# A block of halved products and its plain neighbours: which PSUM banks the plain pair takes, and where the halved pair's last product stands

## The chip, the cores and the metric

The kernel runs on one core of a Trainium2 chip. The metric is device time in microseconds (us) of one launch. Before the change the median of three runs is 963.95 us (963.66 to 964.03). Smaller is better.

TensorE (PE in the profile) multiplies and writes its sums into eight PSUM banks, numbered 0 to 7 here, each 128 partitions by 512 float32. VectorE (DVE) and ScalarE (ACT) read those banks, do the pointwise work and split operands. GpSimd (POOL) and SyncE (SP) mostly issue DMAs in this stretch. Each engine works through its own queue in order.

## The reference, cut to what matters

A decoder block with 512 tokens and 1024 channels: adaLN vector, a Mamba-2 mixer and a pooling mixer, then an MLP. The change touches the MLP alone:

```python
h = rmsnorm(x, norm_mlp_w[i]) * (1.0 + scale_f) + shift_f
x = x + gate_f * (jnp.square(jax.nn.relu(h @ w_up[i])) @ w_down[i])
return rmsnorm(x, norm_final_w)
```

`w_up` is 1024 x 4096 and `w_down` 4096 x 1024, all float32. Channels lie on the partitions and tokens on the free axis, so `h` is 8 blocks of 128 x 512, and the hidden layer 32 such blocks.

## The kernel before, in words

**Precision.** A float32 operand is split into a high part in a rounded format (`fp32r`) and a low part, the difference. A block product is then three matmuls: high by high, high by low, low by high (`mm3`, L154 to L158, and `product`, L870 to L874). The split is `two` (L835): a cast on ScalarE (L837), then a subtraction on VectorE (L838). Weights are split as they arrive, activations as they are made.

**Quarters.** The hidden layer is worked through in four quarters q = 0 to 3 of 8 blocks. In each, "up" jobs make the eight hidden blocks `us[0]` to `us[7]` (ReLU L1087, square L1088, split), and "down" jobs multiply them by `w_down` and add into the residual `x1`.

**Plain jobs and pairs.** A `Plain` job multiplies weight units as they are. A `Pair` job makes two output blocks at once by a Strassen-Winograd scheme over 2 x 2 halves: seven products of 12 matmuls of 256 columns (L874) in place of eight, with sums of weight parts S1 to S4 and sums of activation parts T1 to T4. A pair's products, by method:

- `lead` or `first`: A11·B11 into its accumulator bank `ac` (and A12·B21 ahead of it in a led pair, one that follows a plain job)
- `open`: S1·T1; `middle`: S2·T2, then VectorE adds (L971), and A12·B21; `third`: S3·T3, then VectorE adds (L978) from the left half of `ac` into its right half
- `close`: S4·B22, which completes the pair's first output block and hands it to `done(0, ...)`; then A22·T4 onto the left half of `ac`, which completes the second block, `done(1, ...)`, and frees `ac`

A22·T4 writes where the add of `third` reads, so it waits for L978. For an up pair `done` is `activated` (L1082): ReLU, square, split into `us`, and after the second block the T sums (L840 to L851) for the down pairs.

**Order of jobs** (L1228 to L1240): `up_first` (four plain up units), four plain up units (`up_plain`); then for every q a plain down job for output blocks 0 and 1 (`down_plain`), down pairs jj = 1 (the led one), 2, 3, and four up pairs for the next quarter. The last quarter ends with down pairs 1 and 2 and a plain job by token halves, `last_down`, for output blocks 6 and 7.

`run_jobs` (L992) writes them out. After a pair, at a plain job, the stream is: the pair's `close` (both products), the preparation of the next job (`prepare`: sum z, L906, and the split of S1 and A11; then `prepare_more`: rest of z, L917, and the split of S2 and S4), the plain job's matmuls, and then `prepare_rest` (the split of S3 and A12, and of A22).

`down_plain` goes over 16 blocks: k = 0 to 5 for its two outputs in turn, then k = 6, 7 for the first output and for the second. `us[6]` and `us[7]`, the last ones made, are thus read from the 13th block on.

**PSUM.** Banks 4 to 7 hold the pairs' first outputs, banks 0 and 1 (`AC`) the pairs' `ac`, banks 2 and 3 (`PU`) the plain jobs' sums. `up_first` uses 0, 1, 5 and 7; the four `up_plain` units take 2, 3, 2, 3; every `down_plain` takes 2 and 3. `Slots` hands out the longest free.

**SBUF slots.** Split weights lie in nine slots `HL`. The led pair's low part of S3 and A12 is written where the plain job's first unit had its high part, so that subtraction waits until TensorE is through with that unit's last block.

**The planner.** The stream is not issued as written. A planner places each engine's instructions in a queue beforehand: of those that are ready by its own estimates of durations, the one written first goes first, and work under `tc.high_priority()` ahead of that (the adds L971 and L978, DMAs, the split of plain units). `tc.issue_after(ins)` keeps an instruction behind `ins` on its engine. `mids` (L1080) lists the adds L971 and L978 as they are written.

Of the kernel before, what the change touches and what calls it, by code (L numbers as in the profile page):

```python
# [13 lines left out]
T = 512  # L14
# [48 lines left out]
def block_kernel(tc, xp, crow, arow, par, adaT, wstart, wz, wx, wpool_in, wgate, wpw, wbs, wbp, wout, wup, wdn, out):  # L63
# [3 lines left out]
    with (  # L67
# [764 lines left out]
        ut = [[[raws[p][:, 2 * i + k, :].bitcast(F32R) for k in range(2)] for i in range(2)] for p in range(2)]  # L832
        Y4S = Slots(lambda i, dt: slots("pad", 1, (P, T + 16), first=APART[i][0]).get(dt)[:, APART[i][1]:APART[i][1] + T], 4)

        def two(src, dst):  # L835

            act.copy(dst[0], src)  # L837
            dve.tensor_tensor(dst[1], src, dst[0].bitcast(F32), ALU.subtract)  # L838

        def sums(u1, u2, ts):  # L840

# [34 lines left out]
        class Pair:  # L876
# [17 lines left out]

            def keep(self, y, *names):
                hl = HL.get(F32R), HL.get(F32R)
                two(y, hl)
                for n, o in zip(names, (0, T)):
                    self.a[n] = tuple(x[:, o:o + T] for x in hl)
                    self.left[n] = hl  # L900

            def prepare(self):
                ya = self.y[0]
                self.a, self.left = {}, {}
                z = Z.get()
                dve.tensor_tensor(z[:, :T], ya[:, :T], ya[:, T:], ALU.add)  # L906
                if self.led:
                    yb = self.y[1]
                    dve.tensor_tensor(yb[:, :T], yb[:, :T], ya[:, T:], ALU.add)
                self.keep(ya, "S1", "A11")  # L910
                RL.put(ya)
                self.z = z
# [68 lines left out]
            def close(self):  # L981
                self.mul(self.c12, "S4", "B22")
                self.done(0, (self.c11, self.c12), 1)
                BE.put(self.be)
                self.mul(self.ac[:, :H], "A22", "T4")
                self.done(1, (self.ac,), -1)
                AC.put(self.ac)
# [4 lines left out]
        def run_jobs(jobs):  # L992

            last, todo = None, list(jobs)

            def pump():
                while todo and len(RL.free) >= todo[0].raws and (not isinstance(todo[0], Pair) or Y4.free):
                    todo.pop(0).fetch()

            pump()  # L1000
            jobs[0].prepare()
            pump()
            for n, job in enumerate(jobs):
                after = jobs[n + 1] if n + 1 < len(jobs) else None

                def ahead():
                    if after:
                        after.prepare()
                    pump()

                def more():
                    if isinstance(after, Pair):
                        after.prepare_more()

                def rest():
                    if isinstance(after, Pair):
                        after.prepare_rest()
                    pump()

                if isinstance(job, Pair):  # L1020
                    if not isinstance(jobs[n - 1], Pair):
                        if job.led:
                            job.lead()
                        else:
                            job.first()
                        job.open()
                    else:
                        job.first()
                    if last:
                        last.close()  # L1030
                    ahead()
                    job.middle()
                    more()
                    if isinstance(after, Pair):
                        after.open()
                    job.third()
                    last = job
                    rest()
                else:
                    if last:  # L1040
                        last.close()
                    last = None
                    ahead()
                    more()
                    job.run()
                    rest()
                    if job.after:
                        job.after()
                        pump()
# [49 lines left out]
        class Plain:  # L1099
# [10 lines left out]
                for u in self.units:  # L1110
                    u.prepare()

            def run(self):
                self.body([u.w for u in self.units])
                for u in self.units:
                    u.done()

        def up_first(w):

            ps = [AC.get(), AC.get(), banks[1], banks[3]]  # L1120
            for t0, t1 in HALVES:
# [31 lines left out]

        def up_plain(p, i):

            def f(w):
                ps = PU.get()
                for k in range(8):
                    mm3(ps, w[0][k], h2[k], k == 0, k == 7)
# [14 lines left out]

        def down_plain(q, js):

            def f(w):
                if q == 3 and 0 in js:
                    free([t for m in h2t for t in m])
                    sq.extend([S.get(), S.get()])  # L1180
                n = len(js)
                ps = [PU.get() for _ in js]
                order = [(k, i) for k in range(6) for i in range(n)] + [(k, i) for i in range(n) for k in (6, 7)]
                for k, i in order:
                    mm3(ps[i], w[i][k], us[k], k == 0, k == 7)
                for i, j in enumerate(js):
                    dve.scalar_tensor_tensor(x1[j], ps[i], mod[:, 40 + j:41 + j], x1[j], ALU.mult, ALU.add)
                    if q == 3:
                        squares(j)
                PU.put(*ps)  # L1190
            return Plain(loads(q, js), f)

        def loads(q, js):
# [11 lines left out]
                    squares(j)  # L1205
            return Pair(wdn[4 * jj + q], ub, f, jj == 1)

        def last_down(w):
            js = (6, 7)
            PU.free = [2, 3, 6, 7, 1, 0, 4, 5]  # L1210
            for t0, t1 in HALVES:
                for j in js:
                    ps = PU.get()
                    for k in range(8):
                        mm3(ps[:, t0:t1], w[j - 6][k], us[k], k == 0, k == 7, t0, t1)
                    x = x1[j][:, t0:t1]
                    dve.scalar_tensor_tensor(x, ps[:, t0:t1], mod[:, 40 + j:41 + j], x, ALU.mult, ALU.add)
                    squares(j, t0, t1, int(j == 7))
# [100 lines left out]
```

## Time and profile before

| | before |
|---|---|
| median of three runs | 963.95 us |
| the profiled execution, its own time | 962.53 us |
| its span, first to last instruction | 960.8 us |
| TensorE busy | 939.9 us (98%) |
| VectorE busy | 724.5 us (75%) |
| ScalarE busy | 542.5 us (56%) |
| mean granted TensorE clock | 0.995 |

All figures but the median are of one execution. "Busy" is the union of an engine's instructions; matmuls overlap, so a busy TensorE may still be slower than it could be, and its pace is read from the distance between starts. In a timeline row come the start, the duration, engine, line, operation, tiles (out<-in), the shape, and in brackets how long the engine sat idle before it and what ended that. Rows of equal instructions in a row are merged (xcount); the shape is then that of the first. In a row of windows come the stretch and its length, then for each engine its busy time and number of instructions, the granted TensorE clock, and the share and rate of the DMA engines.

### The profile page before, as it was taken

The numbers are of one execution on the slowest core, as the hardware profiler recorded it, in microseconds if no ns is written. First come the engines' busy times: TensorE is split into PE (matmuls) and PEld (weight loads), VectorE is DVE, ScalarE is ACT, GpSimd is POOL, SyncE is SP. The second block draws the span as 40 slices with busy tenths as digits, with TensorE's granted clock in tenths as the row PEclk, the third lists the DMA queues.
The fourth block names the chain that finished last, engine by engine and source line by source line (L and its number), as shares of the span: only waits on it lengthen the run. The fifth ranks groups of instructions, "written<-read, shape, count | busy, mean of one in ns | idle before, by whom it ended". The sixth has DMA issues, their size and how long they took to land.

```text
span 960.8 us, 14381 instructions
## 1 busy us (share of the span) xinstructions
PE 939.9 (98%) x5503; PEld 811.3 (84%) x5503; DVE 724.5 (75%) x1125; ACT 542.5 (56%) x893; POOL 126.1 (13%) x133
## 2 busy tenths in 40 slices
PE   8999999999999999999999999998999999999996
PEld 4777888888888888787888888996999899899896
DVE  7978868467766787987577565787769888977984
ACT  6479975667538542563412352585458547646853
POOL 0102321220312132300000000001111111111100
PEclk9999999999999999999999999999999999999998
DMA  9847333433253334446578364044586675676612
GB/s 364 304 133 186 124 102 121 132 111 110 75 158 113 98 106 131 154 154 200 179 262 278 119 210 132 23 114 106 134 201 153 149 195 148 164 188 174 169 30 88
DMA packets 70935, 146.34 MB, mean 152 GB/s; under 512 B 5521, under 2 KB 30353, under 8 KB 70866
## 3 DMA queue, kind: packets, MB, share of 16 engines
q1 hardware_dynamic: 64816, 134.41, 43.9%
q0 software_dynamic: 6048, 11.01, 7.5%
q8 instruction: 43, 0.70, 0.3%
q14 instruction: 26, 0.21, 0.1%
q10 hardware_dynamic: 2, 0.00, 0.0%
HBM read 143.17 MB, written 2.23 MB: 151 GB/s over the span
## 4 chain that ended last, share of the span: by engine, by line
PE 73%; DVE 12%; DMA 6%; ACT 5%; issue 3%; POOL 0%; SPq 0%; DVEq 0%; POOLq 0%; ACTq 0%
PE ps L874 17%; PE ps L156 16%; PE ps L158 16%; PE ps L157 16%; PE ps L328 4%; DMA d<-wdn 3%; DMA d<-cs_d 2%; DVE d L147 2%; DVE s L127 1%; PE ps L549 1%; DVE d L838 1%; ACT d L837 1%; DVE pad L631 1%; DVE d L172 1%; PE ps L529 1%
## 5 line engine op out<-in xcount | busy, mean ns | idle before, releaser
L156 PE MATMUL ps<-s,d 128*128 128x512 f32 (+1 forms) x896 | 343.5, 384 | 5.2 <-ACT s L1087 3.8
L157 PE MATMUL ps<-s,d 128*128 128x512 f32 (+1 forms) x896 | 339.2, 379 | 0.2 <-DVE s L127 0.2
L158 PE MATMUL ps<-s,d 128*128 128x512 f32 (+1 forms) x896 | 339.1, 379 | 0.0
L156 PEld LDWEIGHTS ps<-s,d 128*128 128x128 f32 x896 | 168.4, 188 | 40.2 <-ACT s L1087 4.2
L158 PEld LDWEIGHTS ps<-s,d 128*128 128x128 f32 x896 | 168.8, 188 | 32.0 <-issue 0.2
L157 PEld LDWEIGHTS ps<-s,d 128*128 128x128 f32 x896 | 168.6, 188 | 31.1 <-DVE s L127 0.7
L874 PE MATMUL ps<-s,d 128*128 128x256 f32 x1359 | 166.9, 279 | 0.7 <-DVE d L838 0.6
L874 PEld LDWEIGHTS ps<-s,d 128*128 128x128 f32 x1359 | 162.1, 188 | 2.0 <-DVE d L838 1.7
L147 DVE TENSOR_TENSOR d<-d,d 128x1024 fp32r<-128x1024 f32 x88 | 112.3, 1277 | 62.5 <-ACT d L146 57.6
L146 ACT CAST d<-d 128x1024 fp32r<-128x1024 f32 x88 | 92.0, 1046 | 115.5 <-PE ps L157 78.2
L837 ACT CAST d<-d 128x1024 fp32r<-128x1024 f32 x87 | 90.9, 1048 | 67.1 <-DVE d L917 23.7
L838 DVE TENSOR_TENSOR d<-d,d 128x1024 fp32r<-128x1024 f32 x87 | 105.8, 1223 | 25.1 <-PE ps L157 11.6
L172 DVE CUSTOM_DVE_ANT_0 d<-d,d,par_t 128x1024 f32<-128x1024 f32 x32 | 41.8, 1307 | 26.5 <-DMA d<-adaT 26.5
L891 POOL DMA_DIRECT2D d<-wdn x11 | 9.7, 883 | 312.2 <-DMA d<-wdn 261.5
L499 ACT ACTIVATE d<-d,ncs 128x128 f32<-128x128 f32 x128 | 39.9, 391 | 3.7 <-POOL d L495 3.6
L328 PE MATMUL ps<-s,d 128*128 128x512 f32 x168 | 40.1, 391 | 1.9 <-ACT s L316 1.9
L397 DVE SCALAR_TENSOR_TENSOR s<-ps,par_t,s 128x511 f32<-128x511 f32 (+2 forms) x54 | 39.7, 742 | 0.3
L328 PEld LDWEIGHTS ps<-s,d 128*128 128x128 f32 x168 | 31.4, 188 | 9.6 <-ACT s L316 2.4
L126 ACT CAST s<-s 128x512 fp32r<-128x512 f32 x32 | 19.7, 619 | 31.2 <-POOL s L511 18.7
L495 POOL TENSOR_SCALAR_AFFINE_SELECT d<-d 128x1024 f32<-128x1024 f32 x16 | 18.2, 1137 | 88.2 <-ACT cd L492 37.3
L127 DVE TENSOR_TENSOR s<-s,s 128x512 fp32r<-128x512 f32 x32 | 25.8, 808 | 4.6 <-ACT s L126 4.5
L874 PE MATMUL ps<-sz,d 128*128 128x256 f32 x198 | 28.4, 278 | 0.0
(231 smaller groups left out, 1236.5 us busy)
## 6 DMA issues: line engine op xcount, KB each, us to landing
d<-adaT SPq DMA_DIRECT2D x32, 512.0 KB, 4.2
d<-wup SPq DMA_DIRECT2D x32, 512.0 KB, 4.9
d<-wdn SPq DMA_DIRECT2D x32, 512.0 KB, 4.4
d<-wx SPq DMA_DIRECT2D x18, 512.0 KB, 3.6
d<-cs_d SPq DMA_DIRECT2D x16, 512.0 KB, 6.2
d<-wbs SPq DMA_DIRECT2D x16, 512.0 KB, 3.5
d<-wgate SPq DMA_DIRECT2D x16, 512.0 KB, 4.2
d<-wz SPq DMA_DIRECT2D x15, 512.0 KB, 3.7
```

The costliest lines, as they stand in the source:

```text
L146: act.copy(hi[:, :w], r[:, a:a + w])
L147: (low or dve).tensor_tensor(lo[:, :w], r[:, a:a + w], hi[:, :w].bitcast(F32), ALU.subtract)
L156: pe.matmul(ps, whi, xhi[:, t0:t1], start=start, stop=False)
L157: pe.matmul(ps, whi, xlo[:, t0:t1], start=False, stop=False)
L158: pe.matmul(ps, wlo, xhi[:, t0:t1], start=False, stop=stop)
L172: dve.tensor_tensor_reduce(r, r, cbc, 1.0, col("b_ada", j), ALU.mult, ALU.add, mod[:, j:j + 1])
L328: pe.matmul(first[u], w[u][i // 2], h[k][i % 2], start=k == 0 and i == 0, stop=k == 7 and i == 2)
L397: dve.scalar_tensor_tensor(t[:, sh:], ps[:, :T - sh], w(3 - sh), t[:, sh:], ALU.mult, ALU.add)
L499: act.activation(m[:, i, :], m[:, i, :], AF.Exp, bias=ncs[:, c, g * HG + i:g * HG + i + 1])
L837: act.copy(dst[0], src)
L838: dve.tensor_tensor(dst[1], src, dst[0].bitcast(F32), ALU.subtract)
L874: pe.matmul(ps, x, y, start=start and m == 0 and i == 0, stop=m == 3 and i == 2, skip_group_check=True)
```

## The change

1. **Banks.** `down_plain` of q = 0, which follows the plain up units, takes its two banks from `AC` (0 and 1); for q = 1 to 3, after a pair, it takes `PU` (2 and 3) as before.
2. **The pair's close is cut in two.** `close` keeps S4·B22 with `done(0, ...)`; a new `finish` has A22·T4, `done(1, ...)` and the release of `ac`. Between two pairs `finish` follows `close` at once, as before. Where a plain job follows, `finish` is handed to it: `down_plain` calls it after four of its blocks (k = 0 and 1 for both outputs), `last_down` after the eight blocks of its first half output.
3. **Edges.** In a led pair's `prepare` the sum z (L906) and the subtraction of the S1/A11 split are kept behind the newest add in `mids`, which is the add L978 of the up pair just ahead. At q = 0 no pair has run and `mids` is empty, so there is no edge. The cast of the split has none.

```diff
-        def two(src, dst):
+        def two(src, dst, late=None):
             act.copy(dst[0], src)
-            dve.tensor_tensor(dst[1], src, dst[0].bitcast(F32), ALU.subtract)
+            with tc.issue_after(late.ins) if late else nullcontext():
+                dve.tensor_tensor(dst[1], src, dst[0].bitcast(F32), ALU.subtract)
...
             def keep(self, y, *names):
                 hl = HL.get(F32R), HL.get(F32R)
-                two(y, hl)
+                two(y, hl, mids[-1] if mids and self.led else None)
...
                 z = Z.get()
-                dve.tensor_tensor(z[:, :T], ya[:, :T], ya[:, T:], ALU.add)
+                with tc.issue_after(mids[-1].ins) if mids and self.led else nullcontext():
+                    dve.tensor_tensor(z[:, :T], ya[:, :T], ya[:, T:], ALU.add)
...
                 self.mul(self.c12, "S4", "B22")
                 self.done(0, (self.c11, self.c12), 1)
                 BE.put(self.be)
+
+            def finish(self):
                 self.mul(self.ac[:, :H], "A22", "T4")
                 self.done(1, (self.ac,), -1)
                 AC.put(self.ac)
...
                     if last:
                         last.close()
+                        last.finish()
                     ahead()
                     job.middle()
...
                     if last:
                         last.close()
-                    last = None
                     ahead()
                     more()
-                    job.run()
+                    job.run(last.finish if last else None)
+                    last = None
...
-                ps = [PU.get() for _ in js]
+                at = PU if q else AC
+                ps = [at.get() for _ in js]
                 order = [(k, i) for k in range(6) for i in range(n)] + [(k, i) for i in range(n) for k in (6, 7)]
                 for k, i in order:
+                    if between and k == 2:
+                        between()
+                        between = None
                     mm3(ps[i], w[i][k], us[k], k == 0, k == 7)
...
-                PU.put(*ps)
+                at.put(*ps)
...
                     for k in range(8):
                         mm3(ps[:, t0:t1], w[j - 6][k], us[k], k == 0, k == 7, t0, t1)
+                    if between:
+                        between()
+                        between = None
```

`Plain.run`, `up_first`, `up_plain`, `down_plain`'s body and `last_down` get the argument `between` for this.

More of the change, by code (lines that the diff above doesn't have):

```diff
@@ L1111, in prepare, with run, up_first @@
                     u.prepare()
-            def run(self):
-                self.body([u.w for u in self.units])
+            def run(self, between):
+                self.body([u.w for u in self.units], between)
                 for u in self.units:
                     u.done()
-        def up_first(w):
+        def up_first(w, between):
             ps = [AC.get(), AC.get(), banks[1], banks[3]]
@@ L1154, in up_plain, with f @@
         def up_plain(p, i):
-            def f(w):
+            def f(w, between):
                 ps = PU.get()
@@ L1175, in down_plain, with f @@
         def down_plain(q, js):
-            def f(w):
+            def f(w, between):
                 if q == 3 and 0 in js:
@@ L1206, in down, with last_down @@
             return Pair(wdn[4 * jj + q], ub, f, jj == 1)
-        def last_down(w):
+        def last_down(w, between):
             js = (6, 7)
```

## The prediction

> **What bounds the kernel now.** I read the page's busy line and chain first, then TensorE's waits from 608 us on, where the MLP runs, and then the timelines around each wait.
>
> ```profile
> span 960.8 us, 14381 instructions
> PE 939.9 (98%) x5503; PEld 811.3 (84%) x5503; DVE 724.5 (75%) x1125; ACT 542.5 (56%) x893; POOL 126.1 (13%) x133
> PE 73%; DVE 12%; DMA 6%; ACT 5%; issue 3%; POOL 0%; SPq 0%; DVEq 0%; POOLq 0%; ACTq 0%
> ```
>
> TensorE is the bound: 98% busy and 73% of the chain that ended last. A change off it is worth only what it takes out of TensorE's waits.
>
> ```profile
> engine line waited for: us in total, times, longest us
> PE ps L156 <- ACT s L1087: 3.8, 1, 3.8
> PE ps L874 <- DVE ps L978: 3.2, 3, 1.1
> PE ps L874 <- DVE d L838: 0.6, 1, 0.6
> PE ps L778 <- ACT s L1167: 0.5, 1, 0.5
> ```
>
> In 352 us TensorE idles 8.1 us. The first two rows are the places that the diff touches: a plain matmul behind a ReLU, once, and A22·T4 (L874) behind the add L978, three times. The third is an up pair's own A12·B21 and the last the final norm; neither is touched.
>
> **Banks at q = 0.** TensorE's timeline around the long wait, then three windows:
>
> ```profile
> 659.46 0.39 PE L156 MATMUL ps<-s,d 128*128 128x512 f32 x1
> 660.37 0.40 PE L157 MATMUL ps<-s,d 128*128 128x512 f32 x1
> 664.58 0.60 PE L156 MATMUL ps<-s,d 128*128 128x512 f32 x1 [3.81 <-ACT s L1087]
> 676.13 2.99 PE L874 MATMUL ps<-s,d 128*128 128x256 f32 x24
> ...
> 660.00:664.60 4.60, 0.79 (x5) 0.32 (x3) 4.60 (x10) 2.40 (x6) 0.72 (x1) 1.00 0.70 159
> 664.60:668.00 3.40, 3.40 (x9) 2.65 (x10) 3.27 (x8) 2.35 (x4) 0.88 (x1) 0.54 0.67 138
> 745.90:748.00 2.10, 2.08 (x15) 1.99 (x16) 2.10 (x5) 1.55 (x4) 0.84 (x1) 1.00 0.63 95
> ```
>
> The plain down job runs from 659.46 to the led pair's first product at 676.13. Its second output wants bank 3, which the last up unit filled and whose ReLU (L1087) comes late. After the wait the granted clock is 0.54 for 3.4 us and a matmul takes 0.60 us (664.58) and not 0.39 (659.46). At full clock they start 0.229 us apart: at q = 1, shown below, 46 of them lie between 747.44 and 757.98. The job's 48 matmuls would then end at 659.46 + 48 x 0.229 = 670.46. So 5.67 us are lost, 3.98 in the gap (664.58 - 660.37 - 0.23) and 1.69 at the low clock. Banks 0 and 1 have been free since `up_first`, so this wait goes. What is late next:
>
> ```profile
> 663.62 0.40 ACT L837 CAST s<-s 128x256 fp32r<-128x256 f32 x1 [1.58 <-DVE s L842]
> 663.93 0.59 ACT L1087 ACTIVATE s<-ps 128x512 f32<-128x512 f32 x1
> 666.68 1.03 DVE L838 TENSOR_TENSOR s<-s,s 128x512 fp32r<-128x512 f32 x2
> 668.52 0.88 DVE L838 TENSOR_TENSOR s<-s,s 128x256 fp32r<-128x256 f32 x2
> 674.73 1.23 DVE L838 TENSOR_TENSOR d<-d,d 128x1024 fp32r<-128x1024 f32 x1 [5.33 <-PE ps L157]
> 675.87 1.40 DVE L1187 SCALAR_TENSOR_TENSOR xs<-ps,mod,xs 128x512 f32<-128x512 f32 x2
> ```
>
> The ReLU is late because ScalarE, in order, stood behind a cast that waited for VectorE; the change leaves that as it is. `us[7]` has its low part at 666.68 + 0.69 = 667.37, whatever TensorE does. Its first use is the second matmul of the 14th block, 659.46 + 40 x 0.229 = 668.62: 1.25 us to spare. Next is the low part of the led pair's A12, the row at 674.73. It waits for TensorE to leave its slot, 1.40 us ahead of 676.13, so then at 669.06. VectorE is through with the T sums at 668.52 + 0.88 = 669.40, so it runs to 670.63, and the lead's third matmul wants it at 670.46 + 0.24 = 670.70. Last, bank 0 goes on to the led pair's A11·B11: the first eviction L1187 would end near 671.4, and that product starts 12 matmuls of 0.118 us (24 in 2.83 us, at the end of the kernel, below) after the lead, at 671.9. All three fit, by 1.25, 0.07 and 0.5 us. **I take the whole 5.67 us**; bounds 2.5, if one of these chains slips by some 3 us in the new plan, and 5.67.
>
> The 1.69 us counts only if the low clock comes from the gap. The windows say so: 1.00 ahead, 0.54 right behind 3.8 us of idleness, but 1.00 behind the 1.03 us wait at 745.92. Were it otherwise, this part would be 3.98 and the total 1.7 less. The Trainium skill, page "TensorE: Matmul & The Clock Gate", Part 1, states that about 3.4 us of idleness puts the array at half clock and about 3.4 us of work restores it. By that rule any gap left shorter than this costs its own length alone; the trace agrees with its 3.8 and 1.03 us.
>
> **`finish` behind four blocks, q = 1 to 3.** TensorE at q = 1, then VectorE and two rows of ScalarE, then the windows of VectorE's packed stretch at q = 1 and q = 2:
>
> ```profile
> 744.51 0.39 PE L157 MATMUL ps<-s,d 128*128 128x512 f32 x1
> 745.92 1.68 PE L874 MATMUL ps<-s,pad 128*128 128x256 f32 x12 [1.03 <-DVE ps L978]
> 747.44 0.40 PE L158 MATMUL ps<-s,d 128*128 128x512 f32 x1
> 757.98 2.99 PE L874 MATMUL ps<-s,d 128*128 128x256 f32 x24
> ...
> 742.40 0.69 DVE L906 TENSOR_TENSOR d<-d 128x512 f32<-128x512 f32 x1
> 743.36 0.69 DVE L838 TENSOR_TENSOR s<-pad,s 128x512 fp32r<-128x512 f32 x1
> 744.30 1.22 DVE L838 TENSOR_TENSOR d<-d,d 128x1024 fp32r<-128x1024 f32 x1
> 745.44 0.43 DVE L978 TENSOR_TENSOR ps<-ps,pad 128x256 f32<-128x256 f32 x1
> 750.72 1.02 DVE L838 TENSOR_TENSOR s<-s,s 128x256 fp32r<-128x256 f32 x2
> 755.08 0.69 DVE L838 TENSOR_TENSOR pad<-pad,pad 128x512 fp32r<-128x512 f32 x1
> 756.58 1.23 DVE L838 TENSOR_TENSOR d<-d,d 128x1024 fp32r<-128x1024 f32 x1 [0.81 <-PE ps L157]
> 747.69 0.59 ACT L1087 ACTIVATE s<-ps 128x512 f32<-128x512 f32 x1
> 748.18 1.04 ACT L837 CAST d<-d 128x1024 fp32r<-128x1024 f32 x1
> ...
> 741.79:755.77 13.98, 12.95 (x75) 11.15 (x74) 13.97 (x27) 9.97 (x19) 2.60 (x3) 1.00 0.68 167
> 823.52:837.49 13.97, 12.92 (x76) 11.12 (x75) 13.97 (x27) 9.95 (x19) 2.60 (x3) 1.00 0.68 170
> ```
>
> A wait costs 745.92 - 744.51 - 0.23 = 1.18 us; three (3.2 us idle in the list of waits), 3.54. The add L978 stands behind the led pair's split (744.30), and ahead of that its z (742.40): the two that the edges move. Behind four blocks, of which two matmuls had run by then (the one at 747.44 is the third of a block), A22·T4 starts at 744.51 + 11 x 0.229 = 747.03, and L978 without the split ends near 744.7. So the wait goes with 2.3 us of cover, and would go even with no edges.
>
> Whether 1.18 us then reach the end is VectorE's matter: it works 13.97 of 13.98 us, and at q = 2 just so. Its next appointment is the led pair's A12 low part (756.58), which today starts 0.81 us after VectorE is free (755.08 + 0.69 = 755.77) and is wanted two matmuls into the lead. With the lead at 757.98 - 1.18 = 756.80 that is 757.04, so it must start by 755.8. If the pack ends at 755.77 still, all 1.18 us are kept. But z leaves 0.6 us at 742.40 (0.69 less the 0.09 by which neighbours overlap) that may stay empty, since the row at 743.36 waits for a cast on ScalarE; then the pack ends at 756.37 and the lead waits 0.6, so 0.58 is kept. Another row could fill it, as the planner takes what is ready. The bounds are 0 (the pack a whole wait later) and 1.18. **I take 0.85 a quarter, 2.55 in all**, between these two readings.
>
> The second half of the up pair's work comes later: A22·T4 ends at 748.6 instead of 747.6, so its ReLU (747.69) and `us[7]` (low part at 750.72 + 1.02 = 751.74) come about 1.0 later, 752.7. The 14th block's second matmul, the job's 41st, wants it at 744.51 + 39 x 0.229 + 1.41 = 754.85: 2.1 us to spare. Behind that ReLU on ScalarE stand the T casts, whose products come after the lead. The moved z and split serve A11 and S1, not read before 758.2; only S1/A11's raw slot, freed up to 1.8 us later (z's 0.6 and its own 1.14), lets a DMA go later on SP's queue. That is the third down pair's first load, not summed until the led pair's seven products have run, 7 x 1.41 = 9.9 us. So I count nothing; with that cover gone it would cost those 1.8 us.
>
> **`finish` in `last_down`.**
>
> ```profile
> 938.18 0.87 PE L874 MATMUL ps<-sz,pad 128*128 128x256 f32 x6
> 939.60 0.28 PE L156 MATMUL ps<-s,d 128*128 128x256 f32 x1
> 945.25 0.59 PE L778 MATMUL ps<-s,ones 128*128 128x256 f32 x2
> 941.62 0.69 DVE L1171 TENSOR_TENSOR s<-s,s 128x512 f32<-128x512 f32 x1 [0.70 <-ACT s L1170]
> ```
>
> A22·T4 at 938.18 waits for nothing, so there is nothing to win. Moved behind one half output (half of 939.60 to 945.25, 2.83 us), its squares' add would end at 941.62 + 0.69 + 2.83 = 945.1, with the other output's half to add behind it, while the norm's L778 wants the sum at 945.25. I charge 0.15; bounds 0 and 0.5.
>
> **Sum**: 5.67 + 2.55 - 0.15 = 8.07, say 8.0. The profiled execution had 962.53 (span 960.8 and 1.7 around it) and goes to 954.5; the median lies 1.42 above it, so 963.95 - 8.0 = **956.0**.
>
> **Rivals.** *All waits go whole*: 5.67 + 3.54 = 9.2, 954.7. For it: one row put into z's place is enough. Against: the pack has no spare. *VectorE takes it back*: it ends a wait later, the three quarters keep nothing, 963.95 - 5.67 = 958.3; the packed windows speak for it. *A chain slips at q = 0*: of the margins 1.25, 0.07 and 0.5 one is missed by 3 us, 5.0 in all, 959.0. *It does not do what it says*: the wait for bank 3 reappears whole for `us[7]` or A12, and 963.9 stays; that needs `us[7]` at 674 in place of 667.4, and no row holds it so long. *Slower*: the last unit's chain is planned behind the preparation. In the stream `finish` now stands behind z, S1/A11 and S2/S4, so on ScalarE two casts of 1.04 and on VectorE two subtractions of 1.14 (744.30 to 745.44) may go first. At q = 1 to 3 `us[7]` slips by up to 4.4, past its 2.1: a wait of 2.3 in place of 1.18, 3.4 lost in all. If the new plan does the same to the last plain up unit at q = 0, 4.4 past 1.25 is 3.15 idle, with 1.69 at the low clock behind it, and 0.8 of the 5.67 is left. Together 963.95 + 3.4 - 0.8 = 966.5. It decides from `us[7]` at 754.85 (q = 1) and 668.62 (q = 0). Against it: most of the preparation is ready, and placed, before that ReLU could start.
>
> **How the numbers follow.** Chances: forecast 0.52, all whole 0.12, VectorE 0.15, slip at q = 0 0.10, no change 0.06, slower 0.05. About 0.2% (1.9 us) is what a measurement tells from no change. The first four are faster, 0.89; then 0.06 and 0.05. The range reaches from below "all whole" to above the slip, 953.6 to 960.0, and leaves out the last two.
>
> **What would show it.** No wait of L156 on L1087 and granted clock 1.00 through the plain job at q = 0, whose 48 matmuls take about 11.0 us; no wait on L978; L906 and the led split behind L978. A wait of the lead's L874 on VectorE's L838 at q = 1 to 3 tells how much VectorE takes back: 0.3 each by my sum, 0 or 1.2 by the rivals. A wait of L156 to L158 on L838 at the 14th block would prove me wrong on `us[7]`.

## The result and the profile after

The changed kernel takes **958.43 us** (median of four runs, 957.45 to 959.96) against 963.99 us for the kernel before beside it (four runs, 963.66 to 965.29). The ratio is 0.9941, with a 95% interval of 0.9922 to 0.9960: 5.7 us less, between 3.9 and 7.5 (5.6 by the medians). The forecast was 956.0, so 8.0 less, and the time lies inside its range of 953.6 to 960.0. Measured again beside the experiments, the changed kernel had a ratio of 0.9924 (0.9904 to 0.9944), 7.3 us less, between 5.4 and 9.3. Two slow executions, one of e1 (1034 us, its only traced one) and one of e2 (4613 us), are left out of all medians, ratios and intervals, and e1's trace isn't read.

The page of the profiled execution, which took 959.38 us, shows the span, the busy line and the shares of the chain that ended last:

```profile
span 957.7 us, 14382 instructions
PE 942.1 (98%) x5503; PEld 813.6 (85%) x5503; DVE 725.1 (76%) x1125; ACT 542.4 (57%) x893; POOL 126.2 (13%) x133
PE 76%; DVE 12%; DMA 5%; ACT 4%; issue 2%; POOL 0%; SPq 0%; DVEq 0%; POOLq 0%; ACTq 0%
```

TensorE is still the bound, with the same 5503 matmuls. Its waits from 605 us on (L874, L838, L978 and L1087 of before are L875, L839, L980 and L1092 now):

```profile
engine line waited for: us in total, times, longest us
PE ps L875 <- DVE d L839: 1.2, 3, 0.5
PE ps L778 <- ACT s L1172: 0.5, 1, 0.5
```

Both rows that the diff aimed at are gone, 3.8 us behind the ReLU and 3.2 us behind the add. One has come in their place: 1.2 us in three waits on VectorE's subtraction. The final norm's 0.5 us stand as they were.

**At q = 0.** A window over the plain down job's 48 matmuls, TensorE's row that ends it, and two rows of VectorE inside it:

```profile
662.41:673.40 10.99, 10.99 (x50) 9.01 (x48) 10.77 (x21) 7.03 (x13) 1.74 (x2) 1.00 0.64 143
673.40 2.99 PE L875 MATMUL ps<-s,d 128*128 128x256 f32 x24
...
669.50 1.03 DVE L839 TENSOR_TENSOR s<-s,s 128x512 fp32r<-128x512 f32 x2
672.14 1.22 DVE L839 TENSOR_TENSOR d<-d,d 128x1024 fp32r<-128x1024 f32 x1
```

The job takes 10.99 us at clock 1.00, where it took 16.67 (659.46 to 676.13): 5.68 us less. `us[7]` has its low part at about 670.2, and the 14th block's second matmul wants it at 662.41 + 40 x 0.229 = 671.57. The led pair's A12 low part is done at 673.36 (672.14 + 1.22), ahead of the third product's start at 673.64. All nine traces with the new banks (this one and those of e4 to e7 and e9 to e12) have 10.99 us here.

**At q = 1.** TensorE at the lead, then rows of VectorE's pack ahead of it:

```profile
753.81 0.40 PE L875 MATMUL ps<-s,d 128*128 128x256 f32 x2
754.67 2.86 PE L875 MATMUL ps<-s,d 128*128 128x256 f32 x22 [0.47 <-DVE d L839]
...
739.04 0.69 DVE L839 TENSOR_TENSOR s<-pad,s 128x512 fp32r<-128x512 f32 x1 [1.09 <-ACT s L837]
740.11 0.68 DVE L839 TENSOR_TENSOR pad<-pad,pad 128x512 fp32r<-128x512 f32 x1
741.64 0.43 DVE L980 TENSOR_TENSOR ps<-ps,pad 128x256 f32<-128x256 f32 x1
752.46 0.68 DVE L908 TENSOR_TENSOR d<-d 128x512 f32<-128x512 f32 x1
753.40 1.22 DVE L839 TENSOR_TENSOR d<-d,d 128x1024 fp32r<-128x1024 f32 x1
```

A22·T4 no longer waits for the add (741.64). But the lead's third matmul waits 0.47 us for A12's low part, which VectorE begins at 753.40 with no gap ahead of it. At q = 2 and 3 the wait is 0.49 and 0.25 us. From the product at 737.89 us on (740.62 before) and from the like ones at q = 2 and 3, a dozen products into the lead, the same 105 products take 18.19, 18.22 and 17.98 us where they took 18.89, 18.71 and 18.95. Without what a quicker pace of some of them saved (0.15 us in each quarter now, 0.21 at q = 2 before; the pace is explained below), the quarters keep 0.55, 0.55 and 0.83 us of the 1.2 us each.

So the change's own places give 5.68 + 1.93 = 7.6 us in this pair of traces. The spans differ by 3.1 only. Two things that the diff doesn't touch make up the difference.

**The start.** Rows of the chain that ended last, from the first 36 us, of the kernel before:

```profile
1.73 5.42 DMA d<-xp
14.57 5.06 PE ps L328 x21
20.10 4.78 PE ps L328 x21
```

The same of the changed kernel:

```profile
1.72 6.90 DMA d<-xp
16.02 6.67 PE ps L328 x21
23.16 4.78 PE ps L328 x21
```

The first transfer took 1.48 us longer. Then 21 products took 6.67 us and not 5.06: the granted clock from 14 to 22 us was 0.79, and 1.00 before. That is 3.06 us (23.16 - 20.10) lost ahead of everything that was changed.

**The pace.** Two windows of 40 us in a stretch of 256-column products in the trace of before:

```profile
845.00:885.00 40.00, 40.00 (x355) 40.00 (x354) 31.05 (x45) 22.30 (x34) 7.37 (x9) 1.00 0.73 182
685.00:725.00 40.00, 40.00 (x342) 40.00 (x341) 31.75 (x46) 22.14 (x34) 6.08 (x7) 1.00 0.74 177
```

And in the changed kernel's:

```profile
845.00:885.00 40.00, 40.00 (x342) 40.00 (x341) 31.76 (x47) 22.13 (x34) 6.11 (x7) 1.00 0.76 179
```

TensorE is busy throughout at clock 1.00, and yet 355 products pass in one window and 342 in another: 0.1133 us or 0.1178 us from start to start, taken product by product. The quick pace saves 1.5 us in 40. The kernel before had it from 822.5 to 826.3 and from 839.7 to 901.1 us, the changed kernel only in three stretches of 3.8 us (from 737.9, 819.0 and 900.2). Counted product by product from 605 us on, against 0.1178 us, it saved 3.0 us before and 0.8 after.

The sum of it: 7.6 less, 0.6 less for the old wait on L838 that is gone too, 3.1 more at the start, 2.2 more by the pace: 2.9, and the spans show 3.1.

### The profile page after: what moved, and what is told of

It is laid out like the page before. It is cut to its first block, busy times and chain, and to the rows that moved or that the text cites. A ratio compares the mean times of both kernels' runs of the same rounds, so it can differ in the third digit from the quotient of the medians.

```text
span 957.7 us, 14382 instructions
## 1 busy us (share of the span) xinstructions
PE 942.1 (98%) x5503; PEld 813.6 (85%) x5503; DVE 725.1 (76%) x1125; ACT 542.4 (57%) x893; POOL 126.2 (13%) x133
## 4 chain that ended last, share of the span: by engine, by line
PE 76%; DVE 12%; DMA 5%; ACT 4%; issue 2%; POOL 0%; SPq 0%; DVEq 0%; POOLq 0%; ACTq 0%
PE ps L875 18%; PE ps L156 17%; PE ps L157 16%; PE ps L158 16%; PE ps L328 4%; DMA d<-wdn 3%; PE ps L549 1%; DVE d L147 1%; DMA d<-cs_d 1%; DVE s L127 1%; DVE s L839 1%; ACT d L837 1%; DVE d L839 1%; PE ps L529 1%; DVE pad L631 1%
## 5 line engine op out<-in xcount | busy, mean ns | idle before, releaser
L875 PE MATMUL ps<-s,d 128*128 128x256 f32 x1359 | 169.2, 280 | 1.3 <-DVE d L839 1.2
L875 PEld LDWEIGHTS ps<-s,d 128*128 128x128 f32 x1359 | 163.7, 188 | 3.2 <-DVE d L839 2.9
L839 DVE TENSOR_TENSOR d<-d,d 128x1024 fp32r<-128x1024 f32 x87 | 105.8, 1222 | 17.6 <-ACT d L837 10.6
L328 PE MATMUL ps<-s,d 128*128 128x512 f32 x168 | 41.7, 403 | 1.9 <-ACT s L316 1.9
L328 PEld LDWEIGHTS ps<-s,d 128*128 128x128 f32 x168 | 32.5, 195 | 10.1 <-ACT s L316 2.4
L875 PE MATMUL ps<-sz,d 128*128 128x256 f32 x198 | 28.7, 279 | 0.0
```

The lines of the kernel that those rows point to most:

```text
L328: pe.matmul(first[u], w[u][i // 2], h[k][i % 2], start=k == 0 and i == 0, stop=k == 7 and i == 2)
L875: pe.matmul(ps, x, y, start=start and m == 0 and i == 0, stop=m == 3 and i == 2, skip_group_check=True)
```

## The experiments

The kernels ran in three groups, each beside the kernel before: e1 to e4 and e7 to e10 on one chip (medians of before 964.98 and 965.58 us), e5, e6, e11 and e12 on another (965.05). "Less" is what the ratio makes of the median before; it can differ by 1 us from the difference of the medians. "Waits" is TensorE's time lost from 605 us on in the profiled execution, start to start beyond 0.1178 us (256 columns) or 0.229 us (512 columns), the low clock included; "pace" is what the quick pace saved there; "start" is the first transfer and the clock from 14 to 22 us. Waits less pace, taken from a kernel's time between the first product counted and the end of its span, leave 346.4 to 346.6 us in every trace of this table, so the two account for what differs there.

| kernel | median us | ratio (95%) | less, us | waits | pace | start |
|---|---|---|---|---|---|---|
| before (profiled first) | 963.95 | | | 14.2 | 3.0 | 5.42, 1.00 |
| changed (the result) | 958.43 | 0.9941 (0.9922 to 0.9960) | 5.7 | 6.0 | 0.8 | 6.90, 0.79 |
| e1 banks | 959.66 | 0.9935 (0.9916 to 0.9954) | 6.3 | | | |
| e2 finish | 963.93 | 0.9986 (0.9970 to 1.0001) | 1.4 | 13.3 | 0.9 | 6.83, 1.00 |
| e3 edges | 961.75 | 0.9959 (0.9943 to 0.9975) | 4.0 | 14.5 | 5.4 | 6.46, 1.00 |
| e4 banks, finish | 958.12 | 0.9922 (0.9908 to 0.9937) | 7.5 | 6.4 | 1.1 | 6.35, 1.00 |
| e9 changed, again | 958.32 | 0.9924 (0.9904 to 0.9944) | 7.3 | 7.5 | 5.3 | 6.31, 0.79 |
| e7 z later | 955.07 | 0.9895 (0.9873 to 0.9916) | 10.1 | 5.3 | 0.6 | 6.78, 0.79 |
| e10 cast later | 956.46 | 0.9909 (0.9896 to 0.9923) | 8.8 | 6.2 | 1.0 | 5.24, 1.00 |
| e8 shorter gap | 963.16 | 0.9973 (0.9958 to 0.9988) | 2.6 | 12.5 | 3.3 | 6.21, 0.79 |
| e12 z later, again | 956.42 | 0.9912 (0.9889 to 0.9934) | 8.5 | 6.5 | 4.3 | 1.00 |
| e11 z and cast later | 954.10 | 0.9885 (0.9866 to 0.9903) | 11.1 | 4.9 | 4.1 | 5.95, 0.79 |
| e5 banks, edges | 956.17 | 0.9904 (0.9886 to 0.9923) | 9.3 | 6.1 | 3.0 | 5.32, 0.79 |
| e6 end put back | 956.81 | 0.9911 (0.9890 to 0.9932) | 8.6 | 6.8 | 2.9 | 4.69, 1.00 |

e12's chain starts with another transfer, so it has no first figure.

### e1: the banks alone

```diff
-                ps = [PU.get() for _ in js]
+                at = PU if q else AC
+                ps = [at.get() for _ in js]
...
-                PU.put(*ps)
+                at.put(*ps)
```

> Part 1 alone: the plain down job at q = 0 takes banks 0 and 1; close is not cut, no edges. Theory (the bank wait and the low clock behind it are one loss, and nothing takes it back): 5.7 us less than before, 958.3; in the profile no wait on the ReLU at q = 0, its 48 matmuls in 11.0 us at clock 1.00, and the three waits of about 1.05 us on the add of the third product as before. Rival (the gap goes but the low clock stays, or another chain takes over): 4.0 us less or fewer, and a granted clock below 1.00 in that stretch or a new wait at the 14th block.

6.3 us less (4.4 to 8.1). The 5.67 us of the prediction's first step lie within it, and 4.0, the rival's, lies just outside. For the trace, the nine others with these banks stand in: 48 matmuls in 10.99 us at clock 1.00, and no wait on the ReLU.

### e2: `finish` behind four blocks alone

The changed kernel with `at = PU` and without the two edges (`two(y, hl)`, and z with no `issue_after`).

> Part 2 alone: close cut in two, A22·T4 behind four plain blocks, no edges, banks as before. Theory (finish alone covers the late add, the edges are not needed for that): no wait on the add; since z and the led pair's split stay in VectorE's early gap, the pack ends earlier and the lead waits less for the A12 low part than the 0.47, 0.49 and 0.25 us of the changed kernel; 2.5 to 3.5 us less than before, 960.5 to 961.5. Rival (the edges carry the gain): a wait on the add stays, under 1 us less than before.

1.4 us less, between 2.9 less and 0.1 more: a miss. The list of waits from 605 us on, without the norm's row:

```profile
PE ps L156 <- ACT s L1091: 4.5, 1, 4.5
PE ps L875 <- DVE d L839: 1.5, 3, 0.7
```

The wait on the add is gone, so four blocks cover it without the edges, as the prediction said. The lead pays 1.5 us in its place, and not less than in the changed kernel, as I had expected with z in its old place. And at q = 0, where this kernel keeps the old banks, the wait behind the ReLU has grown from 3.8 to 4.5 us; what came behind it:

```profile
667.00:670.00 3.00, 3.00 (x8) 2.31 (x7) 2.84 (x7) 1.88 (x5) 0.88 (x1) 0.50 0.34 48
```

The job's 48 matmuls run from 660.64 to 678.61, 17.97 us in place of 16.67. So some 1.3 us of what this part won it lost at q = 0: 0.7 by a plan that put that ReLU later, the rest because the low clock lasted 6.8 us and not 3.4. With the new banks nothing waits there and the loss can't arise: the parts don't add up.

### e3: the edges alone

The changed kernel with `at = PU`, and `last.finish()` right behind `last.close()` as before.

> Part 3 alone: z and the led pair's low part behind the add of the third product; A22·T4 right behind S4·B22 as before, banks as before. Theory (the add is late because the split of 1.14 us and z of 0.6 us stand ahead of it): the add runs about 1 us earlier, the three waits of 1.05 us fall to 0.3 or less; VectorE's later work takes some back at the lead; 1 to 3 us less than before. Rival (the add is late for other work): waits stay near 1 us and the time is that of before.

4.0 us less (2.4 to 5.5), above what I expected. Its trace explains that only in part. The waits from 605 us on are no fewer than before, and those on the add stay above the 0.3 us of the theory:

```profile
PE ps L156 <- ACT s L1093: 3.8, 1, 3.8
PE ps L875 <- DVE d L839: 1.8, 2, 1.2
PE ps L875 <- DVE ps L980: 1.6, 2, 0.9
```

TensorE's rows at q = 1, with VectorE's row and ScalarE's cast behind them:

```profile
741.29 4.27 PE L875 MATMUL ps<-s,d 128*128 128x256 f32 x34 [1.18 <-DVE d L839]
746.31 1.68 PE L875 MATMUL ps<-s,pad 128*128 128x256 f32 x12 [0.76 <-DVE ps L980]
...
743.22 0.69 DVE L839 TENSOR_TENSOR s<-pad,s 128x512 fp32r<-128x512 f32 x1 [1.64 <-ACT s L837]
...
740.62 1.04 ACT L837 CAST d<-d 128x1024 fp32r<-128x1024 f32 x1 [1.81 <-DMA d<-wdn]
```

At q = 0 the gap is that of before, 3.8 us, but the low clock again lasted 6.8 us and the job took 17.49. The quick pace ran from 678 to 731 and from 759 to 820 us and saved 5.4 us. TensorE came early to places where VectorE wasn't ready, and gave some of it back in waits. VectorE itself stood 1.64 us because ScalarE stood behind the led cast, whose transfer was late. That every execution of e3 has so much of the quick pace isn't shown: only one was traced.

### e4: banks and `finish`, no edges

```diff
-                two(y, hl, mids[-1] if mids and self.led else None)
+                two(y, hl)
...
-                with tc.issue_after(mids[-1].ins) if mids and self.led else nullcontext():
-                    dve.tensor_tensor(z[:, :T], ya[:, :T], ya[:, T:], ALU.add)
+                dve.tensor_tensor(z[:, :T], ya[:, :T], ya[:, T:], ALU.add)
```

> Parts 1 and 2 without the edges. Theory (edges only shift VectorE's work and finish covers the add alone): at least as fast as the changed kernel, 5.7 + 2.5 to 3.5 less than before, 954.8 to 955.8 against a kernel before of 964. Rival (edges needed): slower than the changed kernel by 1 us or more, with waits on the add at q = 1 to 3.

7.5 us less (6.1 to 8.9): as fast as the changed kernel, though 0.7 short of what I wrote. Its list of waits, the norm's row left out:

```profile
PE ps L875 <- DVE d L839: 1.4, 4, 0.4
```

No wait on the add without the edges. And the lead waits 0.39, 0.31 and 0.21 us at q = 1 to 3 (the fourth wait is at q = 0), though z and the split stand where they stood before the change. So z's emptied place, from which the prediction took its 0.6 us, isn't needed for the lead's wait.

### e9: the changed kernel again

> The changed kernel once more, beside the others on one chip. Theory (the waits are gone in the plan, the rest is drawn anew in each execution): TensorE shows the same waits of the lead's first A22·T4 product on VectorE, 0.2 to 0.5 us at q = 1 to 3, and none on the ReLU at q = 0, whose 48 matmuls take 11.0 us; but the first x transfer takes nearer 5.4 than 6.9 us, the clock from 14 to 22 us is nearer 1, and the span falls by 2 to 3 us against 957.7; the median lies 957.5 to 959.0, 5.5 to 7 below the kernel before. Rival (start-up and pace are tied to the new order of the work): first transfer 6.9 us, clock 0.8 from 14 to 22 us, span within 0.5 of 957.7, and the fast pace of 0.1133 us per product in the same three stretches.

7.3 us less. A window of 40 us:

```profile
685.00:725.00 40.00, 40.00 (x356) 40.00 (x354) 32.57 (x49) 24.38 (x39) 6.08 (x7) 1.00 0.74 184
```

The same program has the quick pace from 673 to 735 us, where it didn't have it in its first trace. So the pace isn't tied to the order of the work, and the rival falls on it. The start went the rival's way in part: 6.31 us for the first transfer and a clock of 0.79. But e10 and e6, the changed kernel but for one edit, have 5.24 and 4.69 us with clock 1.00, and e8, which is the kernel before but for q = 0, has 6.21 and 0.79. The start is drawn anew too.

Where TensorE is quick, VectorE takes part of it back:

```profile
735.08 4.28 PE L875 MATMUL ps<-s,d 128*128 128x256 f32 x34 [0.63 <-DVE d L839]
752.49 1.74 PE L875 MATMUL ps<-s,d 128*128 128x256 f32 x13 [0.70 <-DVE d L839]
```

The first is a wait of A12·B21, 0.04 us in the first trace, the second the lead's, 0.70 in place of 0.47. The 0.6 us that the kernel before waited on L838 are such a wait too: they end its quick stretch at 902 us.

### e7, e12: z behind the led pair's last subtraction

```diff
-                with tc.issue_after(mids[-1].ins) if mids and self.led else nullcontext():
+                late = mids[-1] if mids and self.led else leds.pop() if leds else None
+                with tc.issue_after(late.ins) if late else nullcontext():
```

`leds` holds the led pair's A12 subtraction, so the z of the pair that is prepared next (752.46 at q = 1 above) goes behind it. By the order of jobs this is the second down pair, and not an up pair, as the expectation has it.

> The changed kernel with the next up pair's z held behind the led pair's last subtraction (A12's low part). Theory (VectorE's pack sets the lead): z's 0.60 us leave the pack ahead of A12's low part, so the lead's waits of 0.47, 0.49 and 0.25 us go and the time is 1.0 to 1.4 us below the changed kernel on this chip; no new wait. Rival (A12's low part is set by its slot and the casts, not by the pack): the waits stay, 0 to 0.3 less. Second rival (z is then late itself): a wait of the next up pair's A11·B11 or A12·B21 on VectorE of 0.3 to 1 us appears, and the time is the same or 1 to 2 us above.

> The kernel with z held behind the led pair's A12 low part once more, beside the next ones on one chip. Theory (its 0.6 us leave VectorE's pack ahead of the lead): 9 to 11 us below the kernel before again, so a median of 954 to 956.5; the lead's waits at 0 to 0.4 us. Rival (its first run was a draw of good paces): 7 to 8 us below the kernel before, as the changed kernel was on this chip.

10.1 us less (8.1 to 12.3), then 8.5 (6.4 to 10.7). In e7's trace the lead's waits are 0.0, 0.40 and 0.14 us in place of 0.47, 0.49 and 0.25, which is 0.7 us; the 3 us between its median and e9's are more than its trace shows. In e12's trace, with the quick pace, the lead waits 0.25 and 0.84 us at q = 1 and 3. So the edit does what it says, only in part, and its worth over the changed kernel isn't settled by the two runs.

### e10, e11: the led pair's cast behind the last ReLU

```diff
-            act.copy(dst[0], src)
+            with tc.issue_after(behind.ins) if behind else nullcontext():
+                act.copy(dst[0], src)
```

`behind` is, for the led pair's S1 and A11, the newest ReLU of the up pair that is written by then. With `finish` handed on, that is the one of its first output, `us[6]`, and not its last. The aim is that ScalarE doesn't stand for their transfer while VectorE waits for it (the 1.09 us ahead of 739.04).

> The changed kernel with the led pair's S1/A11 cast held on ScalarE behind the up pair's last ReLU, so that ScalarE doesn't stand 1.25 us for that pair's transfer and VectorE isn't without work for 1.09 us at 737.95. Theory: VectorE's pack gains up to 1.09 us, the lead's waits (0.47, 0.49, 0.25) go, and the time is about 1.2 us below the changed kernel. Rival (the idle 1.09 us is filled with waiting for something else, since VectorE's next rows hang on TensorE's slots): the lead's waits stay within 0.1 and the time is within 0.5. Second rival (the later cast frees its raw slot later and the down pair's load with it): a wait of a down pair's first product appears, 0.5 to 1.8 us each.

> Both edits together: z held behind the led pair's A12 low part, and the led pair's S1/A11 cast behind the up pair's last ReLU. Theory (both free VectorE ahead of the lead): no wait of the lead's A22·T4 over 0.1 us at q = 1 to 3, and 0 to 1 us below the kernel with z alone. Rival (the cast does nothing for the lead, as its first run alone left waits of 0.47 and 0.43 us): the same time as z alone within 0.7 us, and the lead's waits as there.

e10 alone: 8.8 us less (7.4 to 10.0), but the lead's waits don't go, they are 0.57, 0.47 and 0.43 us at q = 0, 1 and 2. So by the trace the rival held: time won early in the pack isn't passed on to the lead. By the time it didn't, for the median lies 1.9 us below e9's; the trace doesn't show where that would come from, and the intervals overlap.

```profile
PE ps L878 <- DVE d L842: 1.5, 3, 0.6
```

Both edits together, the norm's row left out here and above:

```profile
PE ps L880 <- DVE d L842: 0.6, 1, 0.6
```

No wait at any lead is left in this trace. The one of 0.6 us is an A12·B21 in the quick pace. e11 takes 954.10 us, 11.1 less than before (9.4 to 12.9), and its interval, 0.9866 to 0.9903, lies just under that of e9, the changed kernel on the other chip (0.9904 to 0.9944). e6's, which is the changed kernel but for its end and ran beside e11, overlaps it by little (0.9890 to 0.9932). That e11 beats the changed kernel is thus likely, not shown. It has the lowest median of the kernels here; against z alone on the same chip in the same group it is 2.3 us less by the medians, of which its trace shows 1.1 in the lead's waits.

### e8: a shorter gap at q = 0

The kernel before with one line more:

```diff
+                if q == 0:
+                    order = [(k, i) for i in range(n) for k in range(4)] + order[8:]
```

> The kernel before with one edit: at q = 0 the plain down job runs four blocks of its first output ahead of the second output's, so 9 more matmuls (2.06 us) lie ahead of the wait for bank 3, which falls from 3.8 to about 1.75 us. Theory (the low clock at q = 0 comes from the length of the gap): granted clock 1.00 behind the wait, the job's 48 matmuls at 0.229 us, and 2.06 + 1.69 = 3.75 us less than before. Rival (the low clock comes with any stop at that place): 0.54 for some 3.4 us again, and 2.06 us less than before.

2.6 us less (1.2 to 4.1), an interval that holds both the 3.75 of the theory and the 2.06 of the rival, so the trace decides. TensorE's row behind the gap, then two windows:

```profile
666.46 0.50 PE L156 MATMUL ps<-s,d 128*128 128x512 f32 x1 [2.25 <-ACT s L1087]
...
664.21:667.62 3.41, 1.16 (x5) 0.99 (x6) 3.41 (x7) 2.12 (x4) 0.38 (x1) 1.00 0.62 228
667.62:671.03 3.41, 3.41 (x10) 2.62 (x9) 3.20 (x8) 2.02 (x5) 0.51 (x1) 0.50 0.62 109
```

The gap shrank to 2.25 us and the clock fell all the same: 0.50 for 3.41 us, though it began only 1.2 us after the restart. The job takes 15.11 us, 1.56 less than before, which is just what the gap got shorter. Theory wrong, rival right in this trace: a gap of 2.25 us can cost the low clock too. Whether any gap of this size does is taken up in the last section.

### e5: banks and edges, `finish` right behind `close`

```diff
                     if last:
                         last.close()
+                        last.finish()
...
-                    job.run(last.finish if last else None)
+                    job.run(None)
```

> The changed kernel with finish put back right behind close ahead of the plain down jobs (the banks and the edges stay). Theory (the edges alone take the add's wait only in part, and the four blocks are what covers it): waits of A22·T4 on the add of 0.5 to 0.9 us at two or three of q = 1 to 3, and of A12·B21 on VectorE up to 1.2 us where the pace is fast; 1 to 2.5 us above the changed kernel, so 5 to 6.5 below the kernel before. Rival (with the edges in, the four blocks earn nothing): within 0.7 us of the changed kernel, 7 to 7.5 below the kernel before.

9.3 us less (7.4 to 11.0), as e6, nearly the changed kernel, beside it (8.6): no loss is seen, and the rival holds as far as such intervals can tell.

```profile
PE ps L875 <- DVE d L839: 0.7, 1, 0.7
PE ps L875 <- DVE ps L980: 0.6, 2, 0.4
```

The wait on the add is 0.35 and 0.26 us where it is listed, and no lead waits. With the edges in, the split and z no longer stand ahead of the add, and that alone is nearly enough here. It wasn't in e3, which has the same edges and still waited 1.6 us for the add.

### e6: the end put back

`last.finish()` goes back behind `last.close()` in the last down job alone.

> The changed kernel with finish put back right behind close in the last down job alone. Theory (moved there it wins nothing and costs nearly nothing, 0 to 0.15 us): the stretch from the last A11·B11 to the norm's first product is the same within 0.15 us, the time the same within what can be told. Rival (the squares' add behind it is late): that stretch 0.5 us shorter with finish put back.

8.6 us less; the changed kernel in e9 had 7.3, and the two intervals overlap. TensorE's rows of e6 at A22·T4 and at the norm's first product:

```profile
930.93 0.87 PE L875 MATMUL ps<-sz,pad 128*128 128x256 f32 x6
938.00 0.59 PE L778 MATMUL ps<-s,ones 128*128 128x256 f32 x2
```

And of the changed kernel, where A22·T4 (937.85) follows the first half output, which begins at 935.02:

```profile
935.02 0.28 PE L156 MATMUL ps<-s,d 128*128 128x256 f32 x1
937.85 0.87 PE L875 MATMUL ps<-sz,pad 128*128 128x256 f32 x6
942.12 0.70 PE L778 MATMUL ps<-s,ones 128*128 128x256 f32 x2
...
940.92 1.15 DVE L1176 TENSOR_TENSOR s<-s,s 128x512 f32<-128x512 f32 x2 [0.70 <-ACT s L1175]
```

The same 60 products take 7.07 us in one and 7.10 in the other. The norm finds its sum ready at 942.07, 0.05 us ahead.

## Why the prediction was right or wrong

**Banks at q = 0: right, to 0.01 us in the trace.** 5.68 against 5.67, and e1 alone 6.3 (4.4 to 8.1). The 0.01 is partly luck of the trace at hand: the 10.99 us after are the same in nine traces, but the loss before isn't a fixed one. In e3, with the old banks and the same gap of 3.8 us, the job took 17.49 us, 6.5 more. `us[7]` had 1.4 us to spare where I wrote 1.25. The margin of 0.07 us at A12's low part was as thin as it looked: the changed kernel passes it by 0.28, but e4 waits 0.44 us there and e10 0.57, with the same banks.

**The clock: the conclusion held, the rule drawn beside it didn't.** That the low clock comes from the gap is borne out, for the nine traces with the new banks have neither. But I wrote that by the Trainium skill any gap shorter than about 3.4 us costs its own length alone. e8's 2.25 us gap cost 3.4 us at half clock. The same section of the Trainium skill's page "TensorE: Matmul & The Clock Gate" (Part 1) says that the window in which activity is counted runs freely. In e8 the 3.41 us just ahead of the low clock, 664.21 to 667.62, held 2.25 us of idleness and 1.16 us of work, so such a window needn't be wholly idle. The waits of 1.0 to 1.2 us at q = 1 to 3 never brought the clock down; a stop of 1.9 us at the start did in some executions, and the last section shows in which.

**`finish` behind four blocks: the mechanism right, the term mis-sized.** The wait on the add went, without the edges too (e4), and a wait of the lead on L838 took part of it back. I took 0.85 us kept per quarter, 2.55 in all; the trace keeps 0.55, 0.55 and 0.83, 1.93 in all. The times can't weigh so small a term: e2, with this part alone, had 1.4 less (2.9 less to 0.1 more), and e4 is 1.2 ahead of e1 with intervals that overlap. The lead's waits are 0.47, 0.49 and 0.25 us where I wrote 0.3. The reason that I gave for the loss, z's place left empty, isn't what happens: another split fills it (740.11), and e4, which leaves z where it was, has nearly the same waits. What holds the lead seems to be what stands right ahead of A12's low part: with z behind it and the cast moved, no lead waits in e11's one trace, though neither edit alone (e7 and e12, e10) took the waits away.

**What I didn't see is that the two edits of this step do much the same work.** I reckoned the edges as something the four blocks merely needn't have. e5 shows the reverse in part: with the edges, the four blocks earn nothing that the times can tell. Four blocks took the add's wait away in every trace that has them; the edges alone left 0.6 us of it in e5 and 1.6 in e3.

**The end: 0.15 charged, 0.03 measured** (7.10 against 7.07). The squares' add was ready at 942.07 for a product at 942.12; my working had it 0.15 ahead of that product and charged 0.15 for the half behind it, which isn't seen.

**The sum.** 8.07 was forecast and 7.6 is seen at the change's own places. What the step from there to the median left out are the start and the pace, drawn anew in each execution: 3.3 us between the best and the worst start of these traces (the second row of products at 19.89 us in e10 and at 23.16 in the changed kernel), 0.6 to 5.4 us saved by the pace. They fell against the changed kernel in its profiled execution and left 3.1 of it. Over the runs they blur the result: 5.7 in the first measurement, 7.3 in the second. The forecast of 8.0 lies within the second interval and a little outside the first. Whether the change, by taking waits away, also changes how often the quick pace comes is open: thirteen traces with shares of the quick pace from 3% to 49% don't tell.

**The rivals.** VectorE takes it back: in part, 1.2 us of 3.2, not all. A slip at q = 0, no change, slower: none was seen. All whole: e11's trace, where no lead waits, suggests that it could be had.

## What to carry to other kernels

When a long wait of the bounding engine ends on a buffer, look first for a buffer that is free already: the banks, two changed names, brought most of the gain, and they also shielded the kernel from the plan's shifts at that place (e2). Before building a second remedy for the same wait, try each alone, since here the four blocks did the work alone, and the edges much of it. And a stop of TensorE of some 2 us or more must be priced with the low clock that may follow, 1.7 us for each 3.41 us of it here, not by its length alone.

## What the runs showed of the hardware

**Two paces of the same product.** At clock 1.00 and with TensorE busy throughout, 128 x 256 products start either 0.1133 or 0.1178 us apart, 355 or 342 in 40 us, in unbroken runs of 12 to 542 products (1.4 to 61 us). With two exceptions (e3 at 731.2 and e12 at 927 us, where a product or two came late) the pace changes where such a run is broken. That can be a stop for VectorE, if only of 31 to 43 ns, as at the start of the changed kernel's three quick stretches. Or it can be plain 512-column products without any stop, as in the kernel before between A22·T4 (0.1177 us from 827.87 on) and the lead (0.1133 from 839.71 on). Not every such break changes it. The same kernel has it in other places from execution to execution. What decides it isn't known from these runs.

**The start.** The first transfer took from 4.69 to 6.90 us, and the stop of 1.9 to 2.0 us ahead of L328 that every trace has was followed by the low clock in six of thirteen profiles. Either comes without the other. e2 had the long transfer without the low clock:

```profile
1.73 6.83 DMA d<-xp
21.51 4.78 PE ps L328 x21
```

and e5 the short one with it:

```profile
1.73 5.32 DMA d<-xp
21.62 4.78 PE ps L328 x21
```

Each costs 1.4 to 1.5 us at the second row of products (20.10 with neither, 21.51 and 21.62 with one, 23.16 with both).

**Where a stop falls decides, beside its length.** Up to the last products, the granted clock was 1.00 or 0.50, and each low stretch lasted 3.41 us or twice that. Within one trace, the steps of the clock lie whole multiples of 3.413 us apart: e8's first and second low stretch begin at 15.68 and 667.62, which is 191 such steps. So a grid of 3.413 us can be drawn over a trace from any step in it. Windows on that grid around the stop at the start, of the changed kernel:

```profile
12.72:16.13 3.41, 1.48 (x7) 0.50 (x6) 3.37 (x7) 3.02 (x6) 0.00 (x0) 1.00 1.03 404
16.13:19.54 3.41, 3.41 (x9) 2.65 (x10) 3.41 (x7) 1.08 (x2) 0.67 (x1) 0.50 1.03 404
```

and, counted back from the step at 664.84, of the kernel before:

```profile
12.90:16.31 3.41, 1.73 (x8) 1.43 (x9) 3.41 (x6) 2.30 (x4) 0.67 (x1) 1.00 1.03 405
```

In the first the whole stop of 1.9 us lies in one window, TensorE is busy for 1.48 of its 3.41 us, and the clock falls at the window's end. In the second the stop is shared with the window ahead of it, 1.73 us are busy, and the clock stays. From 5 to 940 us, every window at clock 1.00 in the thirteen traces with less than 1.55 us busy is followed by the low clock (e8's 1.16 above too), and none with more. Two lie at the edge itself, with 1.55: e11's is followed by it, e2's is not. This agrees with the freely running window of the Trainium skill's page "TensorE: Matmul & The Clock Gate", Part 1. It would also explain why the same gap of 3.8 us was followed by one low window in the kernel before and by two in e3, where it reached 1.6 us into a second window. That the busy time of the window is what the chip counts is a reading of these traces; no run was made to move a stop along the grid.
